# Output gates of a recurrent mixer as 512-column products ahead of the scan, and score products that alternate between two parities

## The chip, the cores and the metric

One core of a Trainium2 chip runs the whole program in one launch. The metric is the device time of that core in microseconds (us), the median of several runs. Matrix products run on TensorE (PE in the profile, its weight loads PEld), elementwise work on VectorE (DVE) and ScalarE (ACT), DMAs are issued by SyncE (SP) and GpSimd (POOL).

## The reference, cut to what matters

The model is two blocks on a sequence of 512 tokens of width 1024. The second block has a mixer whose one half is a recurrence over tokens with 8 heads of width 64 (width 512 in all), and this is where the change lies:

```python
p = h @ w_in
p_rw = p_rw + (prev - p_rw) * rwkv_mu          # prev: the token before
r, k, v, wd, ad, gd = jnp.split(p_rw, RWKV_SPLITS, axis=-1)
g = jax.nn.sigmoid(gd) @ g2                    # gd: 160 columns, g2: 160 x 512
...
# step of the scan, a state of 64 x 64 for each head
s_kk = jnp.einsum('bhij,bhj->bhi', S, kk_t)
S = S * w_t - s_kk * (a_t * kk_t) + v_t * k_t
y_t = jnp.einsum('bhij,bhj->bhi', S, r_t)
...
y = layer_norm(y, LNX_EPS) * lnx_g + lnx_b
y = (y + bonus) * g                            # g: the output gate
return concatenate([u, y]) @ w_out             # u: a convolution branch, 31 taps
```

All inputs and outputs are 32 bit floats.

## The kernel before, in words

Tokens lie along the free axis: a tile of 128 features x 512 tokens is 128 partitions x 512 columns, four such tiles (f = 0 to 3) hold the 512 features of the recurrence, two heads a tile (one in the lower 64 partitions, one in the upper 64: the two parities).

The mixer (`mixer`) first multiplies the input by `w_in` in the order of the table PH (line 38), each dense product as three products of halves (`mm3`). The last part of PH ends with d0 and d1, the 160 gate columns: 128 of them in the tile `gd[0]`, 32 in `gd[1]`. For d1 a narrow product is made in two steps (`narrow_steps`): four partial sums, a copy on ACT (line 411), then a product with a constant that adds them. Both tiles are then mixed with the token before (lines 1039 on ACT and 1040 on DVE) and get a sigmoid on ACT (line 1225). Beside this last part of PH runs `solve`: 31 steps of two DVE instructions (lines 1163 and 1166) that invert small triangular matrices, then a transposing copy on ACT (line 1173) and two DMAs to DRAM (lines 1174 and 1175).

`scan` then works through the 512 tokens in 8 chunks of 64, two chunks to an index i (0 to 3). For each i there are three lists of items:

- `prep(i)`: loads of the inverses from DRAM (`load`), transposes (`turn`, line 1311), masked scores in four calls of `scores(i, n)` with one PSUM bank each (four products of 64 rows and 128 columns, all with heads of one parity n % 2, so all on the same 64 partitions), a mask product on DVE (line 1329), and two small steps `inverse1` (copy on ACT, line 1339) and `inverse2` (copy on DVE, line 1348).
- `seq(i)`: for each of the two chunks `step1`, `step2` (copies on ACT, lines 1360 and 1366) and `step3` (the new state, on DVE, lines 1380 and 1383): the serial chain of the recurrence.
- `post(i)`: `read`, `norm1`, `norm2`, and `norm3`, which first multiplies the gates of its 128 tokens (for each f a product with 128 rows of g2 and one with 32 rows, 128 columns each, into one bank) and then on DVE adds the bonus (line 1425) and multiplies by the gate, read from PSUM (line 1426); `halves` (lines 355 and 356) splits the result for the output product.

The convolution's 124 taps (line 992, one DVE instruction each) fill DVE between. Seen from the scan, `weave` merges lists in proportion to costs written by hand (`item(1.7, step1, c)` and so on): prep(0) with taps; then seq(i), prep(i+1), post(i-1) and taps for i = 0 to 2; then seq(3) with post(2) and the first output products; then post(3) with the end of the convolution (`conv_mean`, `conv_rstd`, `conv_out`). Behind them come the output products with `w_out`.

What weave fixes is the order in which instructions are written. A scheduler that runs at compile time then orders each engine's instructions: among those that its own timing holds ready, the one written first goes first. So an instruction that waits does not hold those written behind it as long as that timing is right; on the chip each engine runs its list strictly in order. PSUM has 8 banks, taken in turn by `bank()`; a bank is free again when its last reader is done.

Tiles are reused by name: `xt_(k)` gives the 128 x 512 tile x0 to x7. x6 and x7 hold values of `gates` (the a of the recurrence) until `products` (line 1115) has read them, then g2 (two DMAs on POOL's queue, lines 1258 and 1259), and after norm3(3) a part of the output. All matrix products have the line of their helper, 321, in the profile, so groups are told apart by their tiles: `ps<-gd,x` are the gate products, `ps<-ra,kb` the scores, `ps<-dpm,..` the inverse steps, `ps<-x,dpm` step2, `ps<-vt,kbt` step3. A product of 32 bit floats shows as two records of each kind.

Of the kernel before, what the change touches and what calls it, by code (L numbers as in the profile page):

```python
# [15 lines left out]
ALU = mybir.AluOpType  # L16
# [3 lines left out]
P = 128  # L20
T = 512
# [16 lines left out]
PH = "u0 g0 w u1 g1 k0", "k1 k2 k3 r0", "r1 r2 r3 u2 g2", "v0 v1 t0 v2 t1 v3 t2 u3 t3 g3 d0 d1"  # L38
# [201 lines left out]
def weave(*streams):  # L240

    total = [sum(c for c, _ in s) or 1.0 for s in streams]
    done, at = [0.0] * len(streams), [0] * len(streams)
    while True:
        left = [i for i, s in enumerate(streams) if at[i] < len(s)]
        if not left:
            return
        i = min(left, key=lambda i: (done[i] + 0.5 * streams[i][at[i]][0]) / total[i])
        cost, f = streams[i][at[i]]
        at[i] += 1  # L250
        done[i] += cost
        f()
# [3 lines left out]
class Net:  # L256
# [697 lines left out]
    def mixer(self, acc1, acc2, stop):  # L954
        nc, A = self.nc, self.A
# [13 lines left out]
        item = lambda c, f, *a: [(c, lambda: f(*a))]  # L969
        HR = lambda h: slice((h % 2) * 64, (h % 2) * 64 + 64)  # L970
        xt_ = lambda k: self.px.tile([P, T], F32, tag=f"x{k}", name=f"x{k}_{self._n()}")
        with self.phase("mix", False) as pa:
            tile_ = lambda shape, tag, dt=F32, bufs=1: pa.tile(list(shape), dt, tag=tag, name=f"{tag}_{self._n()}", bufs=bufs)
            keep = tile_
            bvt, ust = keep([P, 4, T], "bv"), keep([P, 4, T + 30], "us")
            bv, us = ([t[:, j] for j in range(4)] for t in (bvt, ust))
            gd = [keep([P, T], "gd0"), keep([32, T], "gd1")]
            pcm = keep([P, 8, 4, 2], "pcm")
            nc.gpsimd.memset(pcm, 0.0)
            cv, solved = {}, []  # L980
# [42 lines left out]
            def first():  # L1023
                side = {2 + n: [lambda k=k: self.enter(1, k)] for n, k in enumerate((None, *range(KD)))}
                self.group_halves(A["w_in2k"], 6, xs, room, side, done=lambda m, ps: done(W_IN2[m])(ps), W=2)

            def residual():

                r1 = tile_([P, T], "m")
                self.rstd(acc1, self.c("mean"), r1)  # L1030
                nc.gpsimd.dma_start(dY[KD], r1)
# [14 lines left out]
            def dense(name):  # L1046
                if name == "d1":
                    terms = lambda k: [t.bitcast(F32) for t in xs[k]]
                    return self.narrow_steps(A["w_d1"], terms, lambda: tile_([P, T], "sq", bufs=2), gd_done(1), m=32)
                return self.dense_steps(self.bank, A["w_in2"][W_IN2.index(name) - 6], xs, done(name), split=4)  # L1050

            def done(name):
                if name == "w":
                    return shifted(0, wa)
                return {"k": k_done, "r": r_done, "v": v_done, "u": u_done, "g": ug_done, "d": gd_done}[name[0]](int(name[1]))

            st = {}
# [164 lines left out]
            def gd_done(j):  # L1222
# [3 lines left out]

                return g

            first()
            residual()  # L1230
            ra = [keep([P, 2, T], f"ra{f}") for f in range(4)]
            kb = [keep([P, 8, 2, 64], f"kb{f}") for f in range(4)]
            vt = keep([P, 8, T], "vt")
# [3 lines left out]
            D_ = lambda names: sum([turn(int(n[1])) if n[0] == "t" else dense(n) for n in names.split()], [])  # L1237
            rate = sum([item(0.9, rates, i) + item(0.9, gates, i) for i in range(4)], [])
            solve = item(0.4, solve_start) + sum([item(0.4, solve_step, i) for i in range(31)], []) + item(1, solve_end)
            convs = taps(0) + taps(1) + taps(2) + taps(3)  # L1240
            weave(D_(PH[1]), rate)
            self.log_exp()
            weave(D_(PH[2]), chain)
            weave(D_(PH[3]), solve)
            gains, scratch = (ncg, nlg, ngt, nfg), (dB, dT, dX, dY)
            return self.scan(tile_, xt_, room, ra, kb, bv, vt, gd, pcm, cv, convs, gains, scratch, stop)

    def scan(self, tile_, xt_, room, ra, kb, bv, vt, gd, pcm, cv, convs, gains, scratch, stop):

        nc, A = self.nc, self.A  # L1250
        ncg, nlg, ngt, nfg = gains
        dB, dT, dX, dY = scratch
        item = lambda c, f, *a: [(c, lambda: f(*a))]
        HR = lambda h: slice((h % 2) * 64, (h % 2) * 64 + 64)
        CR = lambda c: slice((c % 2) * 64, (c % 2) * 64 + 64)
        HS = lambda h: slice(h * 64, h * 64 + 64)
        masks, g2, g2b, cen = xt_(5), xt_(6), xt_(7), tile_([P, P], "tiny")
        nc.gpsimd.dma_start(g2, A["g2"][:P])
        nc.gpsimd.dma_start(g2b[:32], A["g2"][P:])
        for t, n in ((masks, "masks"), (cen, "cen")):  # L1260
            p, q = self.cst_at[n]
            nc.gpsimd.dma_start(t, A["cst"][:, p:q])
# [8 lines left out]
        st = {}  # L1271
# [42 lines left out]
            st["kb", c] = t = st["kbt"][:, c % 2]  # L1314
            nc.scalar.copy(t, ps)

        def scores(i, n):

            ps = self.bank()
            sc = tile_([P, T], (f"s{i % 2}", f"s{2 + i % 2}", "di", "kk")[n], bufs=(1, 1, 2, 2)[n])  # L1320
            for m in range(2):
                h = n % 2 + 4 * (n // 2) + 2 * m
                f, R = h // 2, HR(h)
                for q in range(2):
                    ct, k = slice(i * P + q * 64, i * P + q * 64 + 64), 2 * m + q
                    o = ps[:, k * P : (k + 1) * P].rearrange("p (n t) -> p n t", n=2)
                    self.mm(o, kb[f][R, 2 * i + q].rearrange("p n t -> p (n t)"), ra[f][R, :, ct], start=True, stop=True)
                    st["sc", 2 * i + q, h] = sc[:, k * P : (k + 1) * P]
            nc.vector.tensor_mul(sc, ps, masks)

        def inverse1(i):
            ps = self.bank()
# [82 lines left out]

        def norm3(i):
            y4, ti = st["y", i], slice(i * P, (i + 1) * P)
            pg = self.bank()
            for f in range(4):
                fs = slice(f * P, (f + 1) * P)  # L1420
                self.mm(pg[:, fs], g2[:, fs], gd[0][:, ti], start=True, stop=False)
                self.mm(pg[:, fs], g2b[:32, fs], gd[1][:, ti], start=False, stop=True)
            for f in range(4):
                fs, y = slice(f * P, (f + 1) * P), y4[:, f, :]
                nc.vector.scalar_tensor_tensor(y, y, nlg[:, f : f + 1], bv[f][:, ti], op0=ALU.mult, op1=ALU.add)
                nc.vector.scalar_tensor_tensor(y, y, self.v("lnxb", f), pg[:, fs], op0=ALU.add, op1=ALU.mult)
                self.halves(os_[4 + f][0][:, ti], os_[4 + f][1][:, ti], y)

        self.log_exp()
        prep = lambda i: (  # L1430
            item(0.1, load, i) + item(0.4, turn, 2 * i) + (item(0.4, turn, 2 * i + 1) if i < 3 else [])
            + sum([item(0.9, scores, i, n) for n in range(4)], []) + item(1.7, inverse1, i) + item(1.7, inverse2, i)
        )
        seq = lambda i: sum([item(1.7, step1, c) + item(0.9, step2, c) + item(0.9, step3, c) for c in (2 * i, 2 * i + 1)], [])
        post = lambda i: (
            item(1.7, read, 2 * i) + item(1.7, read, 2 * i + 1) + item(0.9, norm1, i) + item(0.9, norm2, i) + item(1.8, norm3, i)
        )
        cut = lambda a: convs[CUT[a] : CUT[a + 1]]
        weave(prep(0), cut(0))
# [7 lines left out]
        if stop == "mix":  # L1447
            for j in range(8):
                t = tile_([P, T], "sq", bufs=2)
# [205 lines left out]
```

## Time and profile before

| | us |
|---|---|
| median of 3 runs | 1715.54 (1696.31 to 1723.81) |
| the profiled execution | 1698.85 |
| its span in the profile, first to last instruction | 1697.0 |
| PE busy / PE weight loads busy | 1668.4 (98%) / 1355.0 (80%) |
| DVE busy / ACT busy | 1023.2 (60%) / 715.4 (42%) |

The profiled execution is 1.85 us longer than its span, and lies 16.7 us under the median. All times inside the program are us from the start of the span. Busy shares are averages over the whole program; matrix products are pipelined and their ends modelled, so a busy PE need not be a PE at its peak. The granted clock of TensorE is shown as a share of 2.4 GHz: 1.00 is 2.4 GHz, 0.50 is 1.2 GHz.

### The profile page before, as it was taken

The page shows a single profiled execution, that of the slowest core. Times are in us where ns is not written, and L with a number is a line of the kernel's source. Part 1 is how long each engine was busy: PE and PEld are TensorE (multiplying, and loading weights), DVE is VectorE, ACT ScalarE, POOL GpSimd, SP SyncE. Part 2 cuts the span into 40 slices and gives each one's busy share as a digit, 9 for nine tenths or more (in the row PEclk, how much of TensorE's full clock was granted, in tenths as well). Part 3 has the DMA queues.
Part 4 walks back from the last instruction along what each step waited for, and adds up shares of the span by engine and source line. Part 5 has one row for each costly group of instructions (what it writes and reads, how often), then busy time and mean ns, then how long its engine had stood idle before and what let it go on. Part 6 is the DMA issues. An engine that isn't in the chain of part 4 may idle for free.

```text
span 1697.0 us, 21883 instructions
## 1 busy us (share of the span) xinstructions
PE 1668.4 (98%) x8644; PEld 1355.0 (80%) x8644; DVE 1023.2 (60%) x1706; ACT 715.4 (42%) x1163; POOL 51.4 (3%) x104
## 2 busy tenths in 40 slices
PE   9999999999999999999999999999999999999997
PEld 7888888877776788888888887778868988888886
DVE  4555555556788565555333479996677676666224
ACT  5423222237678552222322354632347454444222
POOL 0000000000000000000000000000000000000000
PEclk9999999999999999999999999996989999999999
DMA  5344435533210234443233332411033122233332
GB/s 203 123 141 147 146 123 191 169 104 124 63 63 26 75 100 147 144 138 120 96 97 118 112 102 75 112 43 41 17 108 102 60 87 96 92 99 96 95 98 84
DMA packets 63863, 177.17 MB, mean 104 GB/s; under 512 B 17065, under 2 KB 19369, under 8 KB 63760
## 3 DMA queue, kind: packets, MB, share of 16 engines
q1 hardware_dynamic: 52016, 138.96, 25.8%
q0 software_dynamic: 9872, 34.71, 6.5%
q10 hardware_dynamic: 1872, 2.10, 0.4%
q8 instruction: 68, 1.11, 0.3%
q14 instruction: 35, 0.29, 0.1%
HBM read 169.19 MB, written 6.55 MB: 104 GB/s over the span
## 4 chain that ended last, share of the span: by engine, by line
PE 90%; DVE 6%; ACT 2%; DMA 1%; issue 0%; ACTq 0%; SPq 0%; DVEq 0%
PE ps L321 89%; PE ps L869 1%; DVE Ts L1166 1%; DVE Tm L1163 0%; DVE acc L484 0%; DVE wlo L351 0%; DVE f L1600 0%; DVE x L1506 0%; DMA raw<-in_w_in2k 0%; DVE x L1601 0%; DVE x L1507 0%; DMA raw<-in_w_out 0%; PE ps L1311 0%; DVE kb L351 0%; DMA x<-in_x 0%
## 5 line engine op out<-in xcount | busy, mean ns | idle before, releaser
L350 ACT CAST whi<-raw 128x1024 fp32r<-128x1024 f32 (+1 forms) x244 | 249.0, 1021 | 627.9 <-PE ps L321 583.0
L351 DVE TENSOR_TENSOR wlo<-raw,whi 128x1024 fp32r<-128x1024 f32 (+1 forms) x244 | 288.8, 1184 | 255.6 <-ACT whi L350 249.7
L321 PE MATMUL ps<-xh,whi 128*128 128x512 f32 (+1 forms) x1008 | 400.9, 399 | 0.9 <-ACT xh L514 0.9
L321 PE MATMUL ps<-xh,wlo 128*128 128x512 f32 (+1 forms) x1008 | 391.1, 389 | 1.5 <-DVE wlo L351 1.4
L321 PE MATMUL ps<-xl,whi 128*128 128x512 f32 (+1 forms) x1008 | 391.3, 388 | 0.3 <-DVE xl L515 0.3
L321 PEld LDWEIGHTS ps<-xh,whi 128*128 128x128 f32 x1008 | 189.9, 188 | 50.9 <-issue 5.8
L321 PEld LDWEIGHTS ps<-xl,whi 128*128 128x128 f32 x1008 | 189.7, 188 | 43.9 <-issue 5.3
L321 PEld LDWEIGHTS ps<-xh,wlo 128*128 128x128 f32 x1008 | 189.2, 188 | 42.4 <-DVE wlo L351 2.4
L321 PE MATMUL ps<-hh,whi 128*128 128x512 f32 (+1 forms) x560 | 210.5, 376 | 0.0
L321 PE MATMUL ps<-hh,wlo 128*128 128x512 f32 (+1 forms) x560 | 209.8, 375 | 0.0
L321 PE MATMUL ps<-hl,whi 128*128 128x512 f32 (+1 forms) x560 | 209.8, 375 | 0.0
L321 PE MATMUL ps<-oh,whi 128*128 128x512 f32 (+1 forms) x360 | 134.1, 373 | 0.0
L321 PE MATMUL ps<-ol,whi 128*128 128x512 f32 (+1 forms) x360 | 134.0, 372 | 0.0
L321 PE MATMUL ps<-oh,wlo 128*128 128x512 f32 (+1 forms) x360 | 134.0, 372 | 0.0
L321 PEld LDWEIGHTS ps<-hh,whi 128*128 128x128 f32 x560 | 105.4, 188 | 19.6 <-issue 0.8
L321 PEld LDWEIGHTS ps<-hl,whi 128*128 128x128 f32 x560 | 105.4, 188 | 19.0
L321 PEld LDWEIGHTS ps<-hh,wlo 128*128 128x128 f32 x560 | 105.4, 188 | 19.0
L555 DVE TENSOR_TENSOR s<-s,ps 128x512 f32<-128x512 f32 x44 | 30.1, 687 | 132.9 <-PE ps L321 132.9
L321 PEld LDWEIGHTS ps<-oh,wlo 128*128 128x128 f32 x360 | 67.8, 188 | 12.0
L321 PEld LDWEIGHTS ps<-oh,whi 128*128 128x128 f32 x360 | 67.6, 188 | 12.0
L321 PEld LDWEIGHTS ps<-ol,whi 128*128 128x128 f32 x360 | 67.8, 188 | 11.6
L553 DVE TENSOR_TENSOR s<-ps,r 128x512 f32<-128x512 f32 x44 | 30.2, 691 | 73.6 <-PE ps L321 73.6
(441 smaller groups left out, 2211.5 us busy)
## 6 DMA issues: line engine op xcount, KB each, us to landing
raw<-in_ffn_gu SPq DMA_DIRECT2D x82, 512.0 KB, 3.6
ada<-in_ada_w POOLq DMA_DIRECT2D x48, 512.0 KB, 3.9
raw<-in_up SPq DMA_DIRECT2D x38, 512.0 KB, 3.5
raw<-in_ffn_d SPq DMA_DIRECT2D x32, 512.0 KB, 3.5
raw<-in_w_in SPq DMA_DIRECT2D x27, 512.0 KB, 3.6
raw<-in_w_out SPq DMA_DIRECT2D x16, 512.0 KB, 3.6
raw<-in_down SPq DMA_DIRECT2D x16, 512.0 KB, 3.5
raw<-in_ffn_d SPq DMA_DIRECT2D x16, 384.0 KB, 3.0
```

The lines of the kernel that those rows point to most:

```text
L321: self.nc.tensor.matmul(*a, **k)
L350: nc.scalar.copy(hi[:, :n], raw[:, :n])
L351: nc.vector.tensor_sub(lo[:, :n], raw[:, :n], hi[:, :n].bitcast(F32))
L553: nc.vector.tensor_mul(s, pg, r)
L555: self.anchor = nc.vector.tensor_mul(s, s, pu).ins
L869: nc.tensor.transpose(ps[:, i * P : (i + 1) * P], es[u, i][:, j * P : (j + 1) * P], self.c("ident"))
L1166: ins = nc.vector.tensor_add(t[:, i + 1 :, :c], t[:, i + 1 :, :c], o)
```

## The change: what it does

The gates of all 512 tokens are computed before the scan. `gate_load` brings g2 into x6 and x7 ahead of the last part of PH; four items `gate(f)` are added behind d1 in the list that is woven with `solve`, each with two products of 512 columns into a bank of its own; the last of them copies the four banks on ACT into the tiles `gt` (x6, x7 and the tiles of gd0 and gd1, which are all free by then). `norm3` has no matrix product any more and reads the gate from `gt`. `scores(i, g)` now makes two of the old calls at once, with two banks: its products alternate between the two parities, that is between the lower and the upper 64 partitions, and the two mask products follow. The hand-written costs become 1.8 for two items `scores` (they were 0.9 for four) and 0.1 for `norm3` (it was 1.8).

```diff
-            gd = [keep([P, T], "gd0"), keep([32, T], "gd1")]
+            gd, gt = [keep([P, T], "gd0"), keep([P, T], "gd1")[:32]], []
...
+            def gate_load():
+                st["g2"] = xt_(6), xt_(7)
+                nc.gpsimd.dma_start(st["g2"][0], A["g2"][:P])
+                nc.gpsimd.dma_start(st["g2"][1][:32], A["g2"][P:])
+
+            def gate(f):
+                fs, (g2, g2b) = slice(f * P, (f + 1) * P), st["g2"]
+                st["gate", f] = ps = self.bank()
+                self.mm(ps, g2[:, fs], gd[0], start=True, stop=False)
+                self.mm(ps, g2b[:32, fs], gd[1], start=False, stop=True)
+                if f == 3:
+                    gt.extend((xt_(6), xt_(7), keep([P, T], "gd0"), keep([P, T], "gd1")))
+                    for n, t in enumerate(gt):
+                        nc.scalar.copy(t, st["gate", n])
...
-            weave(D_(PH[3]), solve)
+            gate_load()
+            weave(D_(PH[3]) + sum([item(1.7, gate, f) for f in range(4)], []), solve)
...
-        masks, g2, g2b, cen = xt_(5), xt_(6), xt_(7), tile_([P, P], "tiny")
-        nc.gpsimd.dma_start(g2, A["g2"][:P])
-        nc.gpsimd.dma_start(g2b[:32], A["g2"][P:])
+        masks, cen = xt_(5), tile_([P, P], "tiny")
...
-        def scores(i, n):
+        def scores(i, g):
-            ps = self.bank()
-            sc = tile_([P, T], (f"s{i % 2}", f"s{2 + i % 2}", "di", "kk")[n], bufs=(1, 1, 2, 2)[n])
+            ps, sc = [], []
+            for n in (2 * g, 2 * g + 1):
+                ps.append(self.bank())
+                sc.append(tile_([P, T], (f"s{i % 2}", f"s{2 + i % 2}", "di", "kk")[n], bufs=(1, 1, 2, 2)[n]))
             for m in range(2):
-                h = n % 2 + 4 * (n // 2) + 2 * m
-                f, R = h // 2, HR(h)
                 for q in range(2):
                     ct, k = slice(i * P + q * 64, i * P + q * 64 + 64), 2 * m + q
-                    o = ps[:, k * P : (k + 1) * P].rearrange("p (n t) -> p n t", n=2)
-                    self.mm(o, kb[f][R, 2 * i + q].rearrange("p n t -> p (n t)"), ra[f][R, :, ct], start=True, stop=True)
-                    st["sc", 2 * i + q, h] = sc[:, k * P : (k + 1) * P]
-            nc.vector.tensor_mul(sc, ps, masks)
+                    for n in range(2):
+                        h = n + 4 * g + 2 * m
+                        f, R = h // 2, HR(h)
+                        o = ps[n][:, k * P : (k + 1) * P].rearrange("p (n t) -> p n t", n=2)
+                        self.mm(o, kb[f][R, 2 * i + q].rearrange("p n t -> p (n t)"), ra[f][R, :, ct], start=True, stop=True)
+                        st["sc", 2 * i + q, h] = sc[n][:, k * P : (k + 1) * P]
+            for n in range(2):
+                nc.vector.tensor_mul(sc[n], ps[n], masks)
...
         def norm3(i):
-            pg = self.bank()
             for f in range(4):
-                fs = slice(f * P, (f + 1) * P)
-                self.mm(pg[:, fs], g2[:, fs], gd[0][:, ti], start=True, stop=False)
-                self.mm(pg[:, fs], g2b[:32, fs], gd[1][:, ti], start=False, stop=True)
-            for f in range(4):
-                fs, y = slice(f * P, (f + 1) * P), y4[:, f, :]
+                y = y4[:, f, :]
                 nc.vector.scalar_tensor_tensor(y, y, nlg[:, f : f + 1], bv[f][:, ti], op0=ALU.mult, op1=ALU.add)
-                nc.vector.scalar_tensor_tensor(y, y, self.v("lnxb", f), pg[:, fs], op0=ALU.add, op1=ALU.mult)
+                nc.vector.scalar_tensor_tensor(y, y, self.v("lnxb", f), gt[f][:, ti], op0=ALU.add, op1=ALU.mult)
...
-            + sum([item(0.9, scores, i, n) for n in range(4)], []) + item(1.7, inverse1, i) + item(1.7, inverse2, i)
+            + sum([item(1.8, scores, i, g) for g in range(2)], []) + item(1.7, inverse1, i) + item(1.7, inverse2, i)
...
-            ... + item(0.9, norm2, i) + item(1.8, norm3, i)
+            ... + item(0.9, norm2, i) + item(0.1, norm3, i)
```

## Rows read from the trace of the kernel before

**Rows 1.** The page: busy time, then busy tenths and granted clock in 40 slices.

```profile
PE 1668.4 (98%) x8644; PEld 1355.0 (80%) x8644; DVE 1023.2 (60%) x1706; ACT 715.4 (42%) x1163; POOL 51.4 (3%) x104
...
PEclk9999999999999999999999999996989999999999
```

**Rows 2.** Chain that ended last, 1080 to 1290 us: start, us, what.

```profile
1144.93 2.02 ACT Bs L1173
...
1182.94 22.95 PE ps L321 x260
...
1240.30 4.62 DMA raw<-in_w_out
```

**Rows 3.** Windows: length, busy us (count) by engine, PEclk, DMA share, GB/s.

```profile
1142.70:1155.80 13.10, 9.50 (x102) 7.36 (x98) 12.09 (x25) 7.11 (x9) 0.00 (x0) 0.90 0.41 113
1155.80:1182.90 27.10, 27.10 (x210) 24.76 (x209) 12.30 (x19) 4.07 (x7) 0.00 (x0) 0.50 0.06 10
1182.90:1206.70 23.80, 23.80 (x266) 19.55 (x265) 16.17 (x26) 7.39 (x13) 0.00 (x0) 0.93 0.04 7
1206.70:1230.70 24.00, 24.00 (x278) 19.83 (x277) 16.58 (x32) 8.29 (x17) 1.10 (x2) 0.93 0.07 23
1230.70:1271.10 40.40, 38.54 (x298) 26.51 (x297) 30.54 (x59) 19.49 (x37) 3.73 (x7) 0.86 0.34 104
1271.10:1282.50 11.40, 8.39 (x65) 7.77 (x64) 11.40 (x26) 9.00 (x15) 0.00 (x0) 1.00 0.23 75
```

**Rows 4.** Timeline of PE: gate products, and the 512-column constant product.

```profile
1199.56 3.40 PE L321 MATMUL ps<-gd,x 128*128 128x128 f32 x16
...
1249.72 4.13 PE L321 MATMUL ps<-gd,x 128*128 128x128 f32 x16
...
1259.95 1.02 PE L321 MATMUL ps<-x,cst 128*128 128x512 f32 x2
...
1267.86 3.29 PE L321 MATMUL ps<-gd,x 128*128 128x128 f32 x16
```

**Rows 5.** Timeline of PE's weight loads of that product, records of one accumulation.

```profile
1259.53 0.19 PEld L321 LDWEIGHTS ps<-x,cst 128*128 128x128 f32 x1 [0.24 <-issue]
1259.96 0.19 PEld L321 LDWEIGHTS ps<-x,cst 128*128 128x128 f32 x1 [0.24 <-issue]
```

**Rows 6.** Timeline before the scan's first steps; in brackets idle before and releaser.

```profile
1143.58 1.04 PE L321 MATMUL ps<-sq,cst 128*32 128x512 f32 x2 [0.70 <-ACT sq L411]
...
1145.58 2.82 PE L321 MATMUL ps<-ra,kb 64*128 64x128 f32 x32
...
1148.39 0.62 ACT L1225 ACTIVATE gd<-gd 32x512 f32<-32x512 f32 x1
...
1150.04 0.55 PE L321 MATMUL ps<-dpm,s 32*32 32x32 f32 x8 [1.65 <-DMA dpm<-dT]
...
1155.06 0.59 ACT L1315 COPY kbt<-ps 128x512 f32<-128x512 f32 x1 [2.15 <-PE ps L1311]
```

**Rows 7.** Timeline of PE: the 64 x 64 products of `lower`; scores; step2.

```profile
1073.75 0.98 PE L321 MATMUL ps<-kb,ra 64*64 64x64 f32 x32
...
1158.88 3.09 PE L321 MATMUL ps<-ra,kb 64*128 64x128 f32 x16
...
1163.79 2.07 PE L321 MATMUL ps<-ra,kb 64*128 64x128 f32 x8
...
1187.71 1.14 PE L321 MATMUL ps<-x,dpm 64*64 64x64 f32 x16
...
1189.91 1.16 PE L321 MATMUL ps<-ra,kb 64*128 64x128 f32 x8
```

**Rows 8.** Windows of 5 us, columns as in rows 3: where the clock fell.

```profile
1205.00:1210.00 5.00, 5.00 (x62) 4.41 (x60) 3.60 (x9) 1.16 (x3) 0.00 (x0) 0.73 0.01 3
...
1255.00:1260.00 5.00, 5.00 (x23) 2.56 (x20) 1.01 (x4) 1.07 (x4) 1.06 (x2) 0.61 0.34 105
```

**Rows 9.** Timeline of POOL: the loads of g2.

```profile
1090.83 0.51 POOL L1259 DMA_DIRECT2D x<-in_g  x1 [3.95 <-DVE x L1115]
```

More of the change, by code (lines that the diff above doesn't have):

```diff
@@ L1243, in mixer, with scan @@
             weave(D_(PH[2]), chain)
-            weave(D_(PH[3]), solve)
+            gate_load()
+            weave(D_(PH[3]) + sum([item(1.7, gate, f) for f in range(4)], []), solve)
             gains, scratch = (ncg, nlg, ngt, nfg), (dB, dT, dX, dY)
-            return self.scan(tile_, xt_, room, ra, kb, bv, vt, gd, pcm, cv, convs, gains, scratch, stop)
-    def scan(self, tile_, xt_, room, ra, kb, bv, vt, gd, pcm, cv, convs, gains, scratch, stop):
+            return self.scan(tile_, xt_, room, ra, kb, bv, vt, gt, pcm, cv, convs, gains, scratch, stop)
+    def scan(self, tile_, xt_, room, ra, kb, bv, vt, gt, pcm, cv, convs, gains, scratch, stop):
         nc, A = self.nc, self.A
@@ L1435, in scan @@
         post = lambda i: (
-            item(1.7, read, 2 * i) + item(1.7, read, 2 * i + 1) + item(0.9, norm1, i) + item(0.9, norm2, i) + item(1.8, norm3, i)
+            item(1.7, read, 2 * i) + item(1.7, read, 2 * i + 1) + item(0.9, norm1, i) + item(0.9, norm2, i) + item(0.1, norm3, i)
         )
```

## The prediction

> **What bounds the kernel now.** I read the page first. PE is busy for 98% of the span, so only what PE does, or what makes it wait, can count, and its clock is at full nearly everywhere except in the slices around 1145 to 1275 us [rows 1]. That is the scan, the only stretch that the change touches. The chain of waits over it is PE's own work for long pieces, as the 22.95 us without a break from 1182.94; only at its two ends do others stand in it, the copy on ACT behind the solve (2.02 us) and the wait for output weights (4.62 us) [rows 2]. So inside the scan I price PE time, and at its ends waits.
>
> I cut it into stages [rows 3]. A, 1142.7 to 1155.8, is the hand-over from the dense products to the scan: PE busy 9.5 of 13.1 us. B, to 1182.9, is seq(0) with prep(1): PE never idle, at 1.2 GHz throughout (granted clock 0.50). C and D, 23.8 and 24.0 us, are seq(1) and seq(2) with their prep and post: PE never idle, clock 0.93. E, 40.4 us, is seq(3) and the convolution's end at 0.86. F, 11.4 us, has PE waiting again (8.39 busy). Both parts of the change lie in A to F; the rest I leave as it is.
>
> **The change part by part.**
> *Gates taken out of norm3.* Each norm3 issues 16 records of gate products. In C they take 3.40 us, and the same in D (one row stands for both); in E 4.13 us, partly at the lower clock; the fourth, 3.29 us, begins at 1267.86 and ends where F begins [rows 4]. C and D are bound by PE, so 3.4 us go from each. In E 4.1 us go. The fourth is worth nothing: PE idles 3 us in F anyway, waiting for VectorE and ScalarE, whose chain does not pass through the gate. DVE's gate product reads SBUF instead of PSUM, one instruction for one of the same shape: nothing.
>
> *Gates added in A.* Eight products of 512 columns, 16 records. Two such records of one accumulation begin 0.43 us apart at full clock [rows 5], which makes 16 x 0.43 = 6.9 us. The old gates show a surcharge: 16 records of 128 columns in 3.40 us are 0.21 us each, while 8 score records of as many columns take 1.16 us, 0.145 each [rows 4, 7]. What differs is that gates alternate between 128 and 32 rows. The 0.07 x 16 = 1.1 us for eight alternations stays if the new gates alternate as often; so 8.0 us. From above, a whole product takes at most 1.02 us [rows 4]: 8 x 1.02 + 1.1 = 9.3 us.
>
> How much of the 8.0 us is hidden: A has 13.1 - 9.5 = 3.6 us of idle PE [rows 3], such as 0.70 us ahead of the adding product of d1 and 1.65 us before the first inverse step, which waits for the DMA behind the solve [rows 6]. The 128-row products need only gd[0], so they can start in these holes; the 32-row ones need the sigmoid of gd[1], which ends at 1149.0 [rows 6], so they can't run before. Net I take 8.0 - 3.6 = +4.4 us. Lower bound +2, if the following transposes also move into holes. Upper bound: nothing hidden, 9.3, and the four new copies on ACT (0.59 us each, as the copies of 128 x 512 there [rows 6], 2.4 in all) ahead of the copy that the inverse waits for: +11.7. Those copies need all gate products done, since gt takes their operands' tiles; the gates hold four of eight banks until then, and the third and fourth score banks wait for them, which the same 2.4 us covers.
>
> *The loads of g2.* Two DMAs on POOL's queue, before as after; they wait for line 1115 and went out at 1090.83 at the latest, 50 us ahead of the new use [rows 9]. Moving them in the written order changes nothing; what stands behind them on POOL is two memsets of `dpm`, also needed only in A. Nothing.
>
> *Scores in pairs.* For one i there are 32 records. In C and D they come as groups of 8 of one parity, 1.16 us each: 4.6 us for each i [rows 7]. The trace has two rows on what alternating saves. In prep(0), where calls follow each other without other work between, 32 records took 2.82 us [rows 6]: 0.088 a record. And `lower`, whose neighbours go to different halves of the array, took 0.98 us for 32 records of 64 x 64 where step2, all on one part, took 1.14 for 16 [rows 7]: 0.031 against 0.071, a factor 0.43. By the first a pair set takes 2.82, by the second 2.0. I take 2.8, the nearest row: -1.8 us in C and in D, ends 0 and -2.6.
>
> On this the Trainium skill (TensorEngine Tiling, Theoretical Speedup) states up to twice the speed where the contracted dimension is 64 or less. By that rule a set would take 4.6 / 2 = 2.3 us, an estimate from that page, and C and D would each give 0.5 more, a sum of -18.2 in place of -17.2. The trace's nearest row stands at a factor 1.65, short of it, and `lower` with 1 / 0.43 beyond it; the forecast goes by the nearest row.
>
> In prep(0) itself nothing. In B at 1.2 GHz the set takes 3.09 + 2 x 2.07 = 7.2 us, two of whose calls already overlap [rows 7]; at twice 2.82 it would be 5.6: -1.6.
>
> *The clock.* B runs wholly at 1.2 GHz, after a stretch in A with idle PE and small products. After the change PE has 8 us of long products there. The 8-record groups cost 2.07 at the low and 1.16 at the high level [rows 7], a factor 0.56, so B at 2.4 GHz would take 27.1 x 0.56 = 15.2 us, 12 less. But the 32 x 32 inverse steps, with waits for ACT between, still stand right before B, so no row says which level comes. I take half, -6 with the scores' -1.6 on top: -7.6, ends -1.6 and -13. The other falls of the clock, in C at 0.73 and in E at 0.61, come while or right after gates ran [rows 4, 8]; D has one more. Stage means of 0.93, 0.93 and 0.86 are 3.4, 3.4 and 11.3 us at half clock [rows 3]; at full clock these shrink by 0.44: 1.5, 1.5 and 5.0. Half of it for C and D, -0.8 each; in E, where the weights' DMA and the taps on DVE also end waits, -1.
>
> *What is late next.* DVE: it is busy 12.3, 16.2, 16.6 and 30.5 us in B to E, 75.6 of 115.3 [rows 3]. With some 25 us gone it would be 75.6 of 90, in C 16.2 of 18. I give back 2 us for it.
>
> **Sum.** A +4.4; B -7.6; C -3.4 - 1.8 - 0.8 = -6.0; D -6.0; E -4.1 - 1 = -5.1, less 1.1 because a part of E waits for the DMA: -4.0; given back +2. Together -17.2 us. The profiled execution, 1698.85 us, would become 1681.7. It lies 16.7 us under the median of the runs, so for a median like 1715.54 I say 1698.
>
> **The rivals.**
> *The clock holds.* The new long products keep PE at 2.4 GHz through B, and C to E lose their falls. For: every later fall is at a gate. Against: the inverse steps stay. B -13 instead of -7.6, C and D -0.7 more, E -3 more: -27, so 1688. Chance 0.22.
> *Hidden anyway.* PE's relief in C to E meets the recurrence's chain and the taps on DVE. For: DVE at 16.2 of 18 us. Against: taps can move into B, where DVE is idle for 14.8 us. C, D and E would give 2 us each and B 4: +4.4 - 4 - 6 = -6, so 1710. Chance 0.20.
> *The pairs do not overlap,* so that part does not do what it says: -17.2 + 1.8 + 1.8 + 1.6 = -12, so 1704. For: calls of different parity already overlap in part. Chance 0.10.
> *Slower: the gates stand in line.* Nothing of them is hidden, ACT's copies come first (A +11.7), the low clock starts later and so lasts into C. It decides from the point where C runs wholly at 1.2 GHz: (23.8 - 5.2) / 0.56 = 33.2 us, +9.4. With B -1.6, D -5 and E -4: +10.5, so 1726. Chance 0.08.
> Against it: the scheduler may fill the holes, and A ends in small products as before. The Trainium skill (TensorEngine Tiling, Gotcha 1: PSUM Pressure) speaks for it: row tiling raises the pressure on PSUM. By that rule, the pairs, two banks at a time behind four held by gates, would be what waits here; no row of this trace shows a wait for a bank in the scan, so the chance stays small.
>
> **How the numbers follow.** Forecast 0.40, the rivals as given. 2% of 1715.54 is 34 us, about what a measurement of this kernel can tell from no change, and no case reaches it by itself. The three runs of before spread over 27 us, so the medians can add some 10 us to either side: faster by over 2% 0.10, slower by over 2% 0.03, within 0.87. Range: the largest gain, 1688, less 10, to the hidden case, 1710, plus 10: 1678 to 1720. Of the slower rival most is outside; the likeliest case alone spans 1690 to 1707.
>
> **What would show it.** Right: 16 records `ps<-gd,..` of 512 columns between 1142 and 1155, 8 us in all, none later; the first inverse step some 4 us later than 1150.04; C and D each about 18 us, with 32 score records in under 3 us at full clock; clock in C and D at 1.00. Wrong: C and D above 21 us (DVE or the chain took over), scores still 1.16 us for 8, the low clock reaching beyond the state of seq(0), or the inverse step more than 8 us later.

## The result, and the profile after

Timed in turn with the kernel before (20 runs each), the changed kernel takes 1691.61 us in the median against 1702.47, a ratio of 0.993 with a 95% interval of 0.9908 to 0.9951. That is inside the forecast range of 1678 to 1720 and on the side it named, by less than 2%, as was expected with 0.87. Timed a second time, 12 runs against 29, the ratio is 0.9958 (0.9931 to 0.9984). Ratios leave out executions more than 1.5% above the fastest of their kernel, which are one of the changed kernel's, at 3456.67 us, and those of the kernel before at 1721 us and more. The forecast sum was -17.2 us; the medians and the first pair of profiled executions (spans 1697.0 and 1686.1) both show -10.9.

The page of the changed kernel, busy time and granted clock in 40 slices:

```profile
PE 1649.4 (98%) x8596; PEld 1337.2 (79%) x8596; DVE 1022.9 (61%) x1706; ACT 716.9 (43%) x1167; POOL 51.3 (3%) x104
...
PEclk9999999999999999999999999998999999999999
```

PE has 19 us less of busy time than in [rows 1], and one of the two slices below 9 is gone. The windows of the changed kernel at the same landmarks as [rows 3] (chunk 0, 2, 4 and 6 of the recurrence), columns as there, and one of 5 us:

```profile
1142.70:1164.70 22.00, 17.05 (x134) 10.33 (x130) 20.58 (x38) 9.55 (x13) 0.00 (x0) 0.91 0.26 70
1164.70:1182.30 17.60, 16.93 (x194) 15.48 (x194) 10.95 (x18) 3.81 (x7) 0.00 (x0) 0.72 0.07 12
1182.30:1200.00 17.70, 17.03 (x250) 14.49 (x249) 16.15 (x25) 6.71 (x13) 0.00 (x0) 1.00 0.05 9
1200.00:1222.20 22.20, 20.57 (x262) 16.99 (x261) 14.04 (x30) 8.69 (x19) 1.09 (x2) 0.85 0.08 25
...
1175.00:1180.00 5.00, 5.00 (x98) 4.65 (x99) 4.58 (x7) 1.74 (x3) 0.00 (x0) 1.00 0.05 10
```

A went from 13.1 to 22.0 us, B from 27.1 to 17.6, C from 23.8 to 17.7, D from 24.0 to 22.2. Most of B's gain is the clock: 0.72 in place of 0.50. From chunk 6 to the first product of the norm behind the output products it is 78.6 us against 80.8. The timeline of PE in the changed kernel: the gates and what follows them in A, a score set in C, and the waits of D and E (idle before and its releaser in brackets):

```profile
1144.63 3.70 PE L321 MATMUL ps<-gd,x 128*128 128x512 f32 x8
1149.10 3.69 PE L321 MATMUL ps<-gd,x 32*128 32x512 f32 x8 [0.77 <-ACT gd L1225]
1152.72 1.09 PE L1326 MATMUL ps<-cst,kb 128*128 128x128 f32 x8
1153.74 2.06 PE L321 MATMUL ps<-ra,kb 64*128 64x128 f32 x32
1157.03 0.21 PE L321 MATMUL ps<-dpm,s 32*32 32x32 f32 x2 [1.23 <-ACT kbt L1330]
1157.58 0.37 PE L321 MATMUL ps<-dpm,s 32*32 32x32 f32 x6 [0.34 <-DVE s L1349]
1158.84 0.24 PE L321 MATMUL ps<-dpm,di 32*32 32x32 f32 x2 [0.89 <-DVE di L1349]
...
1184.80 1.16 PE L321 MATMUL ps<-ra,kb 64*128 64x128 f32 x16
...
1213.25 1.09 PE L321 MATMUL ps<-Bs,ra 128*64 128x128 f32 x8 [0.96 <-DVE Bs L1403]
1215.01 1.71 PE L321 MATMUL ps<-x,dpm 64*64 64x64 f32 x16 [0.67 <-ACT x L1380]
...
1227.32 0.39 PE L321 MATMUL ps<-oh,kb 128*128 128x256 f32 x1 [1.98 <-ACT oh L355]
...
1249.98 1.12 PE L321 MATMUL ps<-sq,cst 128*128 128x512 f32 x2 [1.98 <-ACT sq L1301]
...
1268.57 0.51 PE L321 MATMUL ps<-oh,kb 128*128 128x256 f32 x2 [2.65 <-ACT oh L355]
```

Three things are to be seen. The sixteen gate records take 3.70 + 3.69 = 7.4 us; the scheduler put the four 128-row products first and the four 32-row ones after them, so nothing alternates. They stand ahead of turns, scores and masks, and idle time as before is still there behind them. And sixteen score records, two parities in turn, take 1.16 us, as long as eight of one parity in [rows 7].

The 1.23 us of idle PE before the first inverse step are put down to the copy `kbt`. That copy stands behind the load of a table and had ended at 1156.28; what ended last is the first mask product on VectorE, 0.67 us from 1156.26:

```profile
1153.92 1.28 ACT L507 ACT_TABLE_LOAD   x1
1155.21 1.07 ACT L1330 COPY kbt<-ps 128x512 f32<-128x512 f32 x2
...
1156.26 1.27 DVE L1349 TENSOR_TENSOR s<-ps,x 128x512 f32<-128x512 f32 x2
```

So the inverse waits for masks, which come late because the scores come late and because taps fill VectorE up to 1156.26.

### The profile page after: what moved, and what is told of

It is laid out like the page before. It is cut to its first block, busy times and chain, and to the rows that moved or that the text cites. A ratio compares the mean times of both kernels' runs of the same rounds, so it can differ in the third digit from the quotient of the medians.

```text
span 1686.1 us, 21795 instructions
## 1 busy us (share of the span) xinstructions
PE 1649.4 (98%) x8596; PEld 1337.2 (79%) x8596; DVE 1022.9 (61%) x1706; ACT 716.9 (43%) x1167; POOL 51.3 (3%) x104
## 4 chain that ended last, share of the span: by engine, by line
PE 89%; DVE 6%; ACT 2%; DMA 1%; issue 0%; ACTq 0%; SPq 0%; DVEq 0%
PE ps L321 88%; PE ps L869 1%; DVE Ts L1166 1%; DVE Tm L1163 0%; DMA raw<-in_w_out 0%; DVE acc L484 0%; DVE wlo L351 0%; DVE f L1615 0%; DVE x L1521 0%; DVE x L992 0%; DVE x L1616 0%; DVE x L1522 0%; DMA raw<-in_w_in2k 0%; DMA x<-in_x 0%; DMA dpm<-dY 0%
## 5 line engine op out<-in xcount | busy, mean ns | idle before, releaser
L351 DVE TENSOR_TENSOR wlo<-raw,whi 128x1024 fp32r<-128x1024 f32 (+1 forms) x244 | 288.9, 1184 | 256.2 <-ACT whi L350 250.2
L553 DVE TENSOR_TENSOR s<-ps,r 128x512 f32<-128x512 f32 x44 | 30.2, 691 | 73.6 <-PE ps L321 73.5
```

Of the source, the lines that this page charges most:

```text
L351: nc.vector.tensor_sub(lo[:, :n], raw[:, :n], hi[:, :n].bitcast(F32))
L553: nc.vector.tensor_mul(s, pg, r)
```

## The experiments

Each profile is one execution, and the first pair of runs showed that the clock has a large share in the difference. So the tables below have three readings of each kernel. First the median and its ratio to runs of the kernel before, taken in turn with it. Then the profiled execution: span, mean granted clock g, and its span at equal clock. The time at 1.2 GHz is 2 x (1 - g) x span, and 0.36 us are taken off for each us of it; that slope comes from the two profiles of before (17.4 us of span for 48.6 us of low clock) and the two of the change (6.2 for 17). Last the mean over all timed executions whose span and clock are known (without those left out of the ratios), brought to 54 us of low clock with the slope that fits them within each kernel, 0.41.

| kernel | median us | ratio (95%) | profile: span, clock | at equal clock | mean of all at 54 us low (executions) |
|---|---|---|---|---|---|
| before | 1702.47 | | 1697.0, 0.984 | 1677.5 | 1693.9 (91) |
| before, again | 1716.13, one run | | 1714.4, 0.970 | 1677.4 | |
| change | 1691.61 | 0.993 (0.9908-0.9951) | 1686.1, 0.989 | 1672.7 | 1692.3 (31) |
| change, again | 1695.20 | 0.9958 (0.9931-0.9984) | 1692.3, 0.984 | 1672.8 | |
| gates only | 1700.74 | 0.9971 (0.9936-1.0005) | 1698.8, 0.982 | 1676.8 | 1694.9 (12) |
| pairs only | 1703.51 | 0.9985 (0.9944-1.0027) | 1700.5, 0.978 | 1673.6 | 1693.2 (12) |
| gates behind prep(0) | 1698.57 | 0.997 (0.9934-1.0006) | 1695.7, 0.984 | 1676.2 | 1695.2 (12) |
| no gates | 1694.36 | 0.9957 (0.9926-0.9989) | 1694.9, 0.981 | 1671.7 | 1689.7 (12) |
| gates split | 1696.84 | 0.9981 (0.995-1.0011) | 1701.0, 0.978 | 1674.1 | 1693.8 (12) |
| fewer taps | 1690.33 | 0.9922 (0.9889-0.9954) | 1696.7, 0.980 | 1672.3 | 1690.9 (12) |
| split, one table | 1688.02 | 0.9916 (0.9887-0.9945) | 1689.0, 0.984 | 1669.5 | 1689.6 (18) |
| the same again | 1688.62 | 0.992 (0.9887-0.9953) | 1686.6, 0.986 | 1669.6 | |
| no gates, one table | 1689.19 | 0.9931 (0.9904-0.9958) | 1691.3, 0.980 | 1666.9 | 1686.9 (7) |
| four row groups | 1686.61 | 0.9914 (0.9883-0.9946) | 1686.0, 0.986 | 1669.0 | 1689.2 (9) |

The clock is shown with three decimals, which leaves +-0.6 us in each equal-clock number. Four profiles need no slope at all, as their clock is 0.984: before 1697.0, gates behind prep(0) 1695.7, change 1692.3, split with one table 1689.0. Over all executions with that clock the mean spans are 1696.4 (10 executions), 1695.9 (3), 1692.6 (2) and 1689.2 (3).

**The two parts alone.** One kernel is the change with the old scores (gates only):

```diff
-        def scores(i, g):
+        def scores(i, n):
...
-            + sum([item(1.8, scores, i, g) for g in range(2)], [])
+            + sum([item(0.9, scores, i, n) for n in range(4)], [])
```

The other is the kernel before with these lines the other way round (pairs only).

> The change with its scores put back into four calls of one parity each; the gates stay ahead of the scan. Theory 1 (the two parts add, each pays for its own PE time): A (time to the first step1) 9 to 10 us longer than before, C shorter by the gates' 3.4 us alone, B shorter by some 6 us where its clock is up, so -2 to -5 us against before, ratio 0.997 to 0.999. Theory 2 (behind the first 20 us the scan is bound by VectorE, so that either part alone already brings what can be had): C and D as short as with both (17.7 and 22.2 us) and -8 us or more, ratio 0.995.

> The kernel before with its scores in pairs of parities; the gate products stay in norm3. Theory 1 (the parts add): A 0.8 us shorter (prep(0)'s 32 records 2.1 in place of 2.8 us), B, C and D 2.4 us shorter each, E 0 to 1 us: -6 to -8 us, ratio 0.995 to 0.9965, so the pairs bring more than the gates. Theory 2 (VectorE bounds C and D): A -0.8, B -2 to -4, C and D under -1 each: -3 to -5 us.

At equal clock the gates alone bring 0.7 us (1677.5 to 1676.8), the pairs alone 3.9, and the change, with both, 4.7: in these single profiles the parts add. By the last column it is +1.0, -0.7 and -1.6, so there the gates alone bring nothing, the pairs little, and the parts do not add; the standard error of a mean of twelve is 0.3 to 0.4 us. The intervals of the ratios are wider than either part. What the change gains apart from the clock is known only as 1.6 to 4.7 us. The gates-only trace says where the expected gain of the gates went. Its gate products and then its windows of C and D, columns as before:

```profile
1145.27 3.70 PE L321 MATMUL ps<-gd,x 128*128 128x512 f32 x8
1149.76 5.11 PE L321 MATMUL ps<-gd,x 32*128 32x512 f32 x8 [0.79 <-ACT gd L1225]
```

```profile
1193.30:1213.60 20.30, 20.30 (x250) 17.23 (x249) 15.22 (x24) 7.29 (x14) 0.00 (x0) 0.92 0.05 8
1213.60:1232.90 19.30, 19.30 (x261) 16.63 (x260) 16.03 (x33) 7.04 (x16) 1.10 (x2) 1.00 0.07 17
```

C is 3.5 us and D 4.7 us shorter than in [rows 3]. Brought to full clock with the forecast's 0.44 us for each us at 1.2 GHz that is 3.5 and 3.1, near the gates' 3.4 each, and B is 0.7 shorter; A, 18.0 us at full clock against 11.0, takes 7.0 of these 7.3 back. Here the clock fell while the 32-row gates ran (5.11 us for what takes 3.69 at full clock), so long products did not hold it up here. The expectation that the gates alone would leave B with a better clock was wrong, and neither theory's gain, 2 to 5 us or 8, was reached.

For the pairs alone, B, C and D:

```profile
1158.50:1181.90 23.40, 22.73 (x194) 20.86 (x193) 11.89 (x19) 3.92 (x7) 0.00 (x0) 0.51 0.07 11
1181.90:1205.10 23.20, 23.20 (x266) 19.04 (x265) 17.11 (x28) 7.37 (x14) 0.00 (x0) 0.86 0.04 7
1205.10:1230.00 24.90, 24.01 (x278) 19.50 (x277) 17.97 (x39) 8.49 (x19) 1.09 (x2) 0.84 0.07 22
```

At full clock they are 2.0, 1.9 and 0.9 us shorter than before, and D has 0.9 us of idle PE that it did not have. Theory 1 expected 2.4 each, theory 2 under 1 in C and D; neither holds in all three.

**Where the gates stand.** In one kernel they come behind the first half's turns, scores and inverse:

```diff
-            weave(D_(PH[3]) + sum([item(1.7, gate, f) for f in range(4)], []), solve)
+            weave(D_(PH[3]), solve)
+            self.gates = sum([item(1.7, gate, f) for f in range(4)], [])
...
-        weave(prep(0), cut(0))
+        weave(prep(0) + self.gates, cut(0))
```

In another the gates are left out:

```diff
-                self.mm(ps, g2[:, fs], gd[0], start=True, stop=False)
-                self.mm(ps, g2b[:32, fs], gd[1], start=False, stop=True)
...
-                        nc.scalar.copy(t, st["gate", n])
+                        nc.gpsimd.memset(t, 0.5)
```

> The change with its gate products written behind the work of the first half (its turns, scores and inverse steps) in place of ahead of it. Theory 1 (A is 8.9 us longer because all of the gates stand in line ahead of turns, scores, masks and inverse, whose waits for ScalarE and VectorE stay idle behind them): the gates fill those waits, A is 3 to 6 us shorter than with the change, and the whole 3 to 6 us below the change, ratio to before 0.990. Theory 2 (the chain from gd through 12 taps and the masks on VectorE sets the first inverse step, wherever the gates stand): A within 1.5 us of the change's, the whole within 2 us of it, ratio 0.993.

> The change without any gate products: the gates are set to 0.5 by GpSimd, so the gates are left out of the computation. It shows what the gates cost where they stand. Theory 1 (nothing of their 7.4 us on PE and of the copies behind them is hidden): A is 8 to 9 us shorter than with the change, the whole 8 to 9 us below it, if the clock behind stays as it is, ratio to before 0.988. Theory 2 (the chain over VectorE sets the first inverse step): A 0 to 3 us shorter, the whole 0 to 3 us below. A third way: without the gates PE's clock is at 1.2 GHz in all of B again, as before; then B is 4 to 6 us longer than with the change and the whole only 3 to 4 us below it.

Behind prep(0) the gates fill no wait: the inverse steps before them keep theirs, and then all but two of the sixteen records run in one piece behind them, at the low clock. Its timeline, and the window:

```profile
1154.54 2.08 PE L321 MATMUL ps<-gd,x 128*128 128x512 f32 x2
...
1157.53 14.09 PE L321 MATMUL ps<-gd,x 32*128 32x512 f32 x14
```

```profile
1153.00:1169.00 16.00, 15.45 (x46) 5.34 (x46) 12.22 (x19) 0.50 (x1) 0.00 (x0) 0.50 0.10 17
```

14 us of long products in one piece did not lift the clock either. Neither theory gave this: the span at the same clock is 3.4 us above the change's.

The kernel without gates came out only 1 us below the change at equal clock, which looked like a proof that they cost nothing. It was none: the groups of ScalarE from 1190 to 1290 us have loads that neither the change nor before has in the scan.

```profile
L499 ACT ACT_TABLE_LOAD x5 | 6.4, 1283 | 0.1
L500 ACT ACT_TABLE_LOAD x5 | 6.4, 1283 | 0.1
```

With the gates gone, gd's last sigmoid was scheduled behind the load of the table for logarithm and exponential, took the table away, and every later pair of the two loaded it anew, ten times 1.28 us. So this run settles nothing, and was mended below.

**The same kernels a second time.** Unchanged, to see whether stage times of one profile can be trusted.

> The changed kernel itself, profiled a second time. In its first profile the clock is at 1.2 GHz for some 12.5 us between the first inverse steps and chunk 1, where the kernel before and the runs with only a part of the change have 28 us or more at that place. Theory 1 (the low stretch belongs to what is issued when): the second profile has it again between about 1162 and 1174 us, within 3 us, and chunk 2's first product within 2 us of 1182.25. Theory 2 (where the low stretch begins and ends differs from one execution to the next): it lies elsewhere by 5 us or more, and the stage times of a single profile are no more than one sample; the median stays near 0.993 of before under both.

> The kernel before itself, profiled a second time. Theory 1: low clock again from about 1154 to 1181.5 us, chunk 2's first product within 2 us of 1182.87. Theory 2: begin or end differ by 5 us or more.

The second theory holds. The change's low stretch, at 1161 to 1174 us in its first profile, now lies at 1152 to 1156 and 1163 to 1186; before's, at 1153 to 1184, now reaches from 1152 to 1230, 78 us in one piece. The same 5-us window in the change's second profile, to be set against 1.00 above, and C of before's second profile in two windows:

```profile
1175.00:1180.00 5.00, 5.00 (x53) 4.52 (x52) 4.10 (x7) 0.58 (x1) 0.00 (x0) 0.50 0.01 3
```

```profile
1184.10:1204.00 19.90, 19.90 (x132) 16.47 (x131) 10.18 (x17) 2.49 (x5) 0.00 (x0) 0.50 0.02 4
1204.00:1224.00 20.00, 20.00 (x136) 15.68 (x135) 6.18 (x11) 4.89 (x8) 0.00 (x0) 0.50 0.02 4
```

PE is busy for all of these 40 us, and for all of the 67 us from 1157, and stays at 1.2 GHz:

```profile
1157.00:1224.00 67.00, 67.00 (x474) 56.89 (x473) 28.65 (x44) 11.44 (x20) 0.00 (x0) 0.50 0.04 6
```

Taken at full clock (0.44 us off for each us at 1.2 GHz, as the forecast had it), the stages do repeat: A 11.0 and 10.5 us before, 19.3 and 18.3 with the change; B 15.2 and 15.2 against 13.3 and 13.2; C 22.3 and 22.3 against 17.7 and 17.7; D 22.4 and 22.4 against 19.2 and 19.2. From chunk 6 to the norm behind the output products it is 75.9 and 73.6 against 74.1 and 73.9. Summed up, the change is 3.2 us shorter in the first pair and 1.7 in the second, nearer to the last column's 1.6 than to the 4.7 that the slope of 0.36 gives.

**The 32-row gates into the waits.** Only these products move, behind the first half's scores:

```diff
             def gate(f):
...
                 self.mm(ps, g2[:, fs], gd[0], start=True, stop=False)
-                self.mm(ps, g2b[:32, fs], gd[1], start=False, stop=True)
+            def gate_rest(f):
...
+                self.mm(st["gate", f], st["g2"][1][:32, fs], gd[1], start=False, stop=True)
...
-            + sum([item(1.8, scores, i, g) for g in range(2)], []) + item(1.7, inverse1, i)
+            + sum([item(1.8, scores, i, g) for g in range(2)], []) + between + item(1.7, inverse1, i)
```

> The change with its four 128-row gate products where they are and its four 32-row ones behind the scores of the first half, ahead of its first inverse step. Theory 1 (the short products stand in line ahead of turns, scores and masks): they now fill the 1.23 and 0.34 us of idle TensorE ahead of the first inverse steps and the scores start 3.7 us earlier, so the scan's first step1 comes 2 to 4 us earlier than with the change, and the whole is 2 to 4 us below the change, ratio to before 0.991. Theory 2 (ScalarE's four copies of gates, 2.4 us, now stand ahead of the inverse's own copy, or VectorE's taps ahead of the masks): first step1 within 1 us of the change's, ratio 0.993. Theory 3 (the clock decides): if the low stretch of B is 28 us as in the runs before, the whole is 4 to 8 us above the change, ratio 0.997.

A came to 20.3 us, 8 of them at the low clock: 16.6 at full clock against 18.3 and 19.3. But this kernel too has the ten table loads, and the whole ended 1.4 us above the change. With the load moved behind prep(0) the question could be put again:

```diff
-        self.log_exp()
         prep = lambda i, between=[]: (
...
         weave(prep(0, self.gates), cut(0))
+        self.log_exp()
```

> The split of the gate products again (128-row ones ahead of the turns, 32-row ones behind the scores), with the load of ScalarE's table for logarithm and exponential put behind the first half's work; in the split before, the sigmoid of gd came behind that load, and ten more loads of 1.28 us followed in the scan. All times here are read at equal clock: from each profile's span 0.36 us is taken off for each us at 1.2 GHz, which puts both profiles of before at 1677.4 and both of the change at 1672.7. Theory 1 (the 32-row products stand in line in A, and what A saves reaches the end): first step1 3 to 4.5 us earlier than with the change at the same clock, the whole at 1668.5 to 1670. Theory 2 (what is saved in A is lost to waits behind it): A as in theory 1, the whole at 1671.5 to 1673.5. Median against before by that 0.992 to 0.995, with the clock as the larger part of its spread.

> The split version with one table load, profiled and timed a second time. Theory 1 (the work in A and not the lie of the clock made its median the lowest): first step1 within 1 us of before's profile when 0.44 us is taken off for each us at 1.2 GHz in A, span at equal clock 1670.5 to 1672, median ratio to before 0.990 to 0.994. Theory 2 (its first timing had a lucky clock): ratio 0.995 or more, as the change's second timing (0.9958) against its first (0.993).

Both profiles give 1669.5 us at equal clock, 3.2 below the change, and both medians lie near 1688. (The last expectation and that of the four row groups below have 1671.3 for this kernel, from another sum of its low clock; here all kernels are compared by the table.) Of theory 1 the A side is to be seen in the timeline of its first profile:

```profile
1148.25 1.04 PE L1331 MATMUL ps<-cst,kb 128*128 128x128 f32 x8
1149.22 2.07 PE L321 MATMUL ps<-ra,kb 64*128 64x128 f32 x32
1151.22 3.69 PE L321 MATMUL ps<-gd,x 32*128 32x512 f32 x8
1154.85 0.43 PE L321 MATMUL ps<-dpm,s 32*32 32x32 f32 x8
...
1157.19 1.91 PE L321 MATMUL ps<-dpm,rf 32*32 32x32 f32 x32 [0.67 <-ACT rf L1364]
```

The masks now run on VectorE while PE is in the 32-row gates, and the inverse starts without the 1.23, 0.34 and 0.89 us of waits. A takes 15.1 us at full clock. The table load moved too, so the two changes are not parted by a run; but in the change the load is not what the inverse waited for, and the first split, with two loads in A, already has 16.6.

**No gates, mended.** The same line moved in the kernel without gates.

> The change without any gate products (the gates are set to 0.5 by GpSimd and so left out of the computation), this time without the ten extra table loads on ScalarE that the first version had in its scan. Theory 1 (A's 8.9 us are the price of the gates and reach the end): span at equal clock 8 to 9 us below the change's 1672.7, so 1664 to 1665. Theory 2 (behind A the scan waits for ScalarE, VectorE and weights, which takes back what PE saves): 1668 to 1672, with more idle PE in C to E than the change has.

The span lies between the two theories, 5.8 us below the change. A takes 11.0 us at full clock, as before the change, so 7.8 us are the gates' price there, and some 2 of them are taken back further on. Against the kernel with pairs only (1673.6), which has the gates in norm3, it is 6.7 us lower. So gates cost 6.7 us in norm3, 5.8 in A as the change has them, and 2.6 in the split form; by the last column 6.3, 5.4 and 2.7. Only the last of these compares kernels with the table load at the same place.

**VectorE.** The last eleven taps are left out:

```diff
-            convs = taps(0) + taps(1) + taps(2) + taps(3)
+            convs = taps(0) + taps(1) + taps(2) + taps(3)[:20] + [(0.65, lambda: None)] * 11
```

> The change without the last 11 of the convolution's 124 taps (they are left out of the computation), 11 x 0.66 = 7.3 us less for VectorE, most of them after the start of the scan's second quarter. Theory 1 (D came out at 22.2 us in place of 18 because VectorE was full from 1200 to 1213 and PE then waited for its Bs and the clock fell): D 2 to 5 us shorter, the whole 2 to 6 us below the change, ratio 0.990. Theory 2 (the fall of the clock in D comes whatever VectorE does): D within 1 us of the change's, the whole within 1.5 us of it.

D in this kernel:

```profile
1212.20:1231.70 19.50, 18.83 (x263) 15.75 (x261) 10.68 (x24) 8.61 (x19) 1.09 (x2) 0.91 0.09 29
```

D takes 18.0 us at full clock in place of 19.2 and has 0.7 us of idle PE in place of 1.6, so the taps are behind the wait for Bs. The whole gains 0.4 us in the profile and 1.4 in the mean of all executions: these taps cost the change 1 us or so, not the 2 to 6 of theory 1.

**Four row groups.** The fold that closes d1 writes gd's last 32 rows four times, and each of the four products uses another group of rows:

```diff
-                    return self.narrow_steps(A["w_d1"], terms, lambda: tile_([P, T], "sq", bufs=2), gd_done(1), m=32)
+                    return self.narrow_steps(A["w_d1"], terms, lambda: tile_([P, T], "sq", bufs=2), gd_done(1))
...
-                self.mm(st["gate", f], st["g2"][1][:32, fs], gd[1], start=False, stop=True)
+                R = slice(f * 32, f * 32 + 32)
+                self.mm(st["gate", f], st["g2"][1][R, :P], gd[1][R], start=False, stop=True)
```

> The split version again, with the four 32-row gate products on four different groups of 32 rows of the array: the fold that ends d1 writes gd's last 32 rows four times, and g2's last rows lie in four blocks. In the scores, neighbours on the two 64-row halves take 0.071 us for each record where neighbours on one half take 0.145. Theory 1 (neighbours on different row groups overlap, by as much as there are groups): the eight records, 3.7 us with all on the first 32 rows, take 1 to 2 us, A is 1.5 to 2.5 us shorter than in the split version if the masks on VectorE do not end its waits, and the span at equal clock is 1668.5 to 1670 against 1671.3. Theory 2 (512-column records are bound by something other than the row group, or the masks end the wait anyway): the records stay at 3 us or more, or A gets back as idle time what they give; the whole within 1 us of the split version.

Its timeline:

```profile
1153.39 1.14 PE L321 MATMUL ps<-gd,x 32*128 32x512 f32 x8
1155.91 0.24 PE L321 MATMUL ps<-dpm,s 32*32 32x32 f32 x2 [1.39 <-DVE s L1357]
```

Eight records of 512 columns take 1.14 us in place of 3.69, a factor of 3.2. Most of it comes back as the wait for the masks, 1.39 us in this row: A takes 14.5 us at full clock against 15.1, and the span at equal clock is 0.5 us below the split version's. The second theory holds for the whole, the first for the records. Its median is the lowest of all, but the split version is not to be told apart from it. Both beat the kernel before by 0.8 to 0.9% and have lower medians than the change.

## Why the prediction came out as it did

The time lies inside the range, and its side was right, but the working gets only a part of the credit. Too much was expected of less work: A was priced too low, E too high. About half of the sum was put down to the clock; a gain of that size is there in the mean, for another reason than was given, and that part is luck.

**Less work.** Without the clock the forecast's terms are A +4.4, B -1.6, C and D -5.2 each, E -3, given back +2: -8.6. At equal clock the profiles show -4.7, the stages at full clock -3.2 and -1.7, the mean over all executions -1.6.

*A, "3.6 us of idle PE hide part of the gates":* this step failed. A is 8 us longer at full clock, not 4.4. The product count was right (7.4 us measured, 8.0 taken; the surcharge for alternating fell away because nothing alternated). But an idle hole is filled only by what stands ahead of it in the engine's list and is ready. The long products were ready early, yet so were the turns and scores they now pushed back, and with these the masks and the inverse, whose waits simply came later. The split version shows it from the other side: with half of the gates behind the scores, 3 to 4 us of A return. The slower rival had it right that nothing of the gates would be hidden. The copies on ScalarE that it put ahead of the inverse were not what the inverse waited for, no row of A puts a wait on the banks of the scores, and the point from which that rival would decide, a C wholly at the low clock, was not reached in either profile of the change.

*Scores, -1.8 for each half:* the mechanism was right and the size too small. A set takes 2 x 1.16 = 2.3 us and not 2.8. The Trainium skill (TensorEngine Tiling, Theoretical Speedup), with its factor of two, had it: 4.64 / 2.32 = 2.0. The forecast's 2.82 came from calls that only overlap at their seams.

*C, -6.0:* it was 6.1 in the first pair, 4.6 of it at full clock where 5.2 were expected; in the second pair, with before's C wholly at 1.2 GHz, it was 22.2, so that the raw 6.1 agrees is chance. *D, -6.0:* it was 1.8 and, at full clock, 3.2. PE waits there 0.96 us for Bs and 0.67 for ScalarE, where it never waited before. That is what the 2 us given back for VectorE stood for; the taps are a part of it. *E, -4.0:* from chunk 6 on, the first pair differs by 2.2 us and the second pair (78.2 and 80.3) by 2.1 the other way; at full clock by 1.8 and by 0.3 the other way. PE's idle time from 1100 to 1320 us is 9.1 us before and 17.5 after, most of the surplus in waits of E for ScalarE, whose copies follow the output weights and the convolution's end. So the rival "hidden anyway" is true of E. Which of these waits binds was not tried.

**The clock.** B's -6 and the falls in C to E made -8.6 of the sum. Over the executions of the last column the mean granted clock is 0.979 before and 0.985 after, 71.6 and 51.1 us at 1.2 GHz: 20.5 x 0.41 = 8.4 us of the 10.1 by which the mean spans differ (1701.1 and 1691.1). The size was right. The reasons were not: gates run through a fall (gates only), long products do not lift it (gates behind prep(0)), and in the change the clock fell again at 1215, 1230 and 1270 us, where no gate runs, so "every later fall is at a gate" was true of one profile only. Gates alone (64 us at 1.2 GHz) and pairs alone (76) do not add to the change's 51.

One thing does go with the place of the gates. The kernel before has a second kind of execution, such as its second profile with 78 us at 1.2 GHz in one piece: in 27 of its 96 later timings the clock is 0.976 or lower and the span 1704 us or more. With the gates in norm3 that is so in 32 of 108 executions (pairs only: 5 of 12), with the gates out of it in 3 of 125, none of the change's 31. That link is seen, not explained: what in the gates' place does it, and why the change's low stretches are shorter than those of the gates alone, stays open.

## What to carry to other kernels

Work put into an engine's idle time must stand in its list between the instruction that the other engine needs first (here the scores) and the one that waits for that engine (here the inverse); ahead of both it only delays the chain. Neighbouring products on different row groups are worth arranging for, as long as the next engine (here VectorE with the masks) keeps up. Where the clock of single executions moves by 10 us and more, compare spans at equal clock, and after any move of work look for new table loads before a run is believed.

## What the runs showed that was not expected

The low stretch of the clock differs between executions of one program: 31 us and 78 us in the two profiles of before, from nearly the same beginning. In these runs PE busy without a gap did not end it: 67 us of small products (B and C of the second profile of before), and 14 us of 512-column ones, ran at 1.2 GHz. With the gates out of norm3 executions at a clock of 0.976 or lower were rare, 3 of 125 against 32 of 108. Four 32-row products on four row groups ran 3.2 times as fast as on one. And leaving out eight matrix products moved one sigmoid behind a table load, which cost ScalarE ten loads of 1.28 us.
